# Two-layer hybrid decoder trunk: most weights of the second layer are split into high and low part by two DMAs each

## The chip, the cores and the metric

The kernel runs on one core of one Trainium2 chip. The metric is the device time of one execution in microseconds, of that one core. The engines are called PE (TensorE), DVE (VectorE), ACT (ScalarE), POOL (GpSimd) and SP (SyncE).

## The reference

All arrays are float32, with 512 tokens and 1024 channels. Each of two layers does x <- x + (1 + gate) * Mixer(RMSNorm(x) * (1 + scale) + shift), with shift, scale and gate from a conditioning vector, and a last RMSNorm follows. Layer 0 mixes by causal pooling and stick-breaking attention. Layer 1, where the change lies, is a gated short convolution:

```python
def odd_mixer(h, w_in, conv_w, conv_b, w_out):
    s = h.shape[1]
    proj = h @ w_in                                        # 1024 -> 8192
    gb, gc, u, gate = jnp.split(proj, [D_CONV, 2 * D_CONV, 3 * D_CONV], axis=-1)
    u = gc * u
    up = jnp.pad(u, ((0, 0), (CONV_WIDTH - 1, 0), (0, 0)))
    conv = conv_b + sum(up[:, j:j + s] * conv_w[j] for j in range(CONV_WIDTH))
    y = gb * conv * jax.nn.silu(gate)
    return y @ w_out                                       # 2048 -> 1024
```

## The kernel before

Channels lie on the 128 partitions and the 512 tokens along the free axis. Every operand of a product is held as two float32r tiles, a high part (the value rounded to float32r) and a low part (the rest). `mm3` (L195) makes one product of three matmuls: high weight by high h, high weight by low h, low weight by high h. A weight unit is a 128x1024 tile, eight 128x128 blocks for one output tile of 128 channels by 512 tokens, so a unit is 24 matmuls of 512 columns.

The weights come as a stream of units in the order in which PE uses them (`units`). `load_upto` (L71) issues the load of a unit into a `raw` tile, a ring of three, from SP. `split_upto` (L78) makes the two parts with `hilo` (L58): ACT casts raw to `whi` (L60) and DVE subtracts it from raw into `wlo` (L61); `whi` and `wlo` are rings of three. `next_unit` (L92) is called when the program comes to a unit's products; it splits two units ahead and loads three ahead. Four units at the start of layer 1 are special: three of them go into tiles that attention no longer needs (`vw`), because their products run together, k outside, first on the tokens 0 to 255 and then on 256 to 511 (`layer1`, L745).

Layer 1 has 80 units. Sixteen blocks j of four units (gc, u, gate and gb: `mtile`, L201) each give one y tile; after block 7 the first half of the output projection follows (8 units, `outproj`), and after block 15 the second half (8 units, `outproj_norm`), whose last two units run by token halves under the statistics of the last norm. In a block ACT copies gc out of PSUM (L768), DVE multiplies it with u into a tile whose 16 leading columns POOL sets to zero (L771, L772), DVE does the convolution (L775, L780), ACT takes the SiLU (L783), DVE multiplies (L785, L786), and the result is split into yh and yl by `hilo`. The product tiles rotate over three PSUM banks.

At the end of layer 0, ACT splits the transposed attention weights (`ah`, `al`) and the y tiles of the pooling branch and of the last heads, and casts the weights of the output projection; then the sums of squares give the scale `u` of the new norm, and ACT and DVE make h of layer 1 by k (`hh` L181, `hl` L184), by token halves.

PE and SP run in program order. On ACT, DVE and POOL, apart from the start and a few marked instructions, a scheduler orders the instructions at build time.

Of the kernel before, what the change touches and what calls it, by code (L numbers as in the profile page):

```python
# [7 lines left out]
F32 = mybir.dt.float32  # L8
# [10 lines left out]
P = 128  # L19
# [6 lines left out]

# columns of the packed small parameters
C_G = 0
# [9 lines left out]
class Trunk:  # L38
    def __init__(self, ctx, tc, io):
        self.tc, self.nc, self.io = tc, tc.nc, io  # L40
        pool = lambda name, bufs, **kw: ctx.enter_context(tc.tile_pool(name=name, bufs=bufs, **kw))
        self.c1 = pool("c1", 1)
        self.wp = pool("wp", 2)
        self.yp = pool("yp", 9)
        self.ap = pool("ap", 1)
        self.tp = pool("tp", 2)
        self.pm = pool("pm", 3, space=PSUM)
        self.pz = pool("pz", 5, space=PSUM)
        self.units = []
        self.loaded = 0  # L50
        self.split_done = 0
        self.used = 0

# [1 line left out]
    def t512(self, tag, n=S, bufs=2):  # L55
        return self.tp.tile([P, n], F32, tag=tag, name=tag, bufs=bufs)

    def hilo(self, hi, lo, src, eng=None, ordered=False):  # L58
        """hi = fp32r(src), lo = src - hi."""
        a = self.nc.scalar.copy(out=hi, in_=src)  # L60
        b = (eng or self.nc.vector).tensor_tensor(out=lo, in0=src, in1=hi.bitcast(F32), op=ALU.subtract)  # L61
        if ordered:
            self.tc.keep_in_program_order(a)
            self.tc.keep_in_program_order(b)

# [1 line left out]
    def add_unit(self, src, cols=1024, lo_eng=None):  # L67
        self.units.append(dict(src=src, cols=cols, lo_eng=lo_eng, dst=None))
        return len(self.units) - 1

    def load_upto(self, n):  # L71
        while self.loaded < min(n, len(self.units)):
            u = self.units[self.loaded]
            u["raw"] = self.wp.tile([P, 1024], F32, tag="raw", name="raw", bufs=3)
            self.nc.sync.dma_start(u["raw"][:, : u["cols"]], u["src"])
            self.loaded += 1

    def split_upto(self, n, ordered=False):  # L78
        while self.split_done < min(n, len(self.units)):
            self.load_upto(self.split_done + 1)  # L80
            u = self.units[self.split_done]
            c = u["cols"]
            if u["dst"] is None:
                hi = self.wp.tile([P, 1024], F32R, tag="whi", name="whi", bufs=3)
                lo = self.wp.tile([P, 1024], F32R, tag="wlo", name="wlo", bufs=3)
            else:
                hi, lo = u["dst"]
            self.hilo(hi[:, :c], lo[:, :c], u["raw"][:, :c], u["lo_eng"], ordered)
            u["w"] = (hi, lo)
            self.split_done += 1  # L90

    def next_unit(self, ahead=2):  # L92
        i = self.used
        self.split_upto(i + 1)
        self.load_upto(i + 3)
        self.split_upto(i + 1 + ahead)
        self.load_upto(i + 4)
        self.used += 1
        return self.units[i]["w"]

# [1 line left out]
    def ada_load(self, layer, part, kt, early=None):  # L102
# [31 lines left out]

# [1 line left out]
    def square(self, kt, sl, out=None):  # L136
# [8 lines left out]
    def rstd(self, ps, rs, sl):  # L145
        """1 / sqrt(ps / D + EPS): a table's estimate and a Newton step."""
        nc = self.nc
        n = sl.stop - sl.start
        y = rs[:, sl]
        nc.scalar.activation(y, ps, AF.Abs_reciprocal_sqrt, bias=self.eps, scale=1.0 / D)  # L150
        v = self.t512("sgp")[:, :n]
        r = self.t512("sgp")[:, :n]
        nc.scalar.activation(r, y, AF.Square)
        if n == S:
            nc.scalar.activation(v, ps, AF.Identity, bias=self.heps, scale=-0.5 / D)
        else:
            nc.vector.tensor_scalar(v, ps, -0.5 / D, -0.5 * EPS, ALU.mult, ALU.add)
        nc.vector.tensor_tensor(out=r, in0=r, in1=v, op=ALU.mult)
        nc.vector.scalar_tensor_tensor(y, r, 1.5, y, ALU.add, ALU.mult)
        return y  # L160

    def warm(self, n):
        """Keep the array busy before the products start, so that its clock is up."""
        ps = self.zbank()
        for _ in range(n):
            self.nc.tensor.matmul(ps, self.zero[:, :P], self.zero, start=True, stop=True)

    def preload_rsqrt(self, after):
        """Bring the table in before the statistics need it."""
        n = after.shape[0]  # L170
# [17 lines left out]
    def make_h(self, layer, kt, rstd, sl):  # L188
        """h = x * rstd * A + m as fp32r halves, A = g * (1 + scale), m = shift."""
        t = self.h_scale(layer, kt, rstd, sl)  # L190
        self.h_hi(layer, kt, t, sl)
        self.h_lo(layer, kt, t, sl)

# [1 line left out]
    def mm3(self, ps, wh, wl, xh, xl, first, last):  # L195
# [5 lines left out]
    def mtile(self):  # L201
        """One [128 channels, 512 tokens] tile of the input projection."""
        wh, wl = self.next_unit()
# [25 lines left out]
    def x_add(self, layer, mt, ps, sl=slice(0, S)):  # L229
        """x += gate * ps."""  # L230
        x = self.x[mt][:, sl]
# [17 lines left out]
    def outproj_norm(self, layer, ys, late=None):  # L249
        """The second half of the output projection, with the sums of squares of the new x.  # L250

        The last two tiles go by token halves, so that the first half's statistics are
        worked out under the products of the second. Returns rstd of the first half and
        a function that gives that of the second.
        """
        acc = []
# [60 lines left out]

# [1 line left out]
    def qk_post(self, ps, which):  # L319
# [21 lines left out]

    # column offsets of the row blocks of the scores and of the transposed weights
    ZOFF = {3: 0, 2: 512, 0: 896, 1: 1024}
    TOFF = {0: 0, 1: 512, 3: 896, 2: 1024}

    def attn_z(self, par):
# [5 lines left out]
        for blocks in ((3,), (2, 0), (1,)):  # L352
# [11 lines left out]
            for i in blocks:  # L364
# [6 lines left out]
                )  # L371
                # running products from the right; they stay 1 where the mask is 1
                r = fw[:, o : o + n][:, ::-1]
                nc.vector.tensor_tensor_scan(r, r, self.mask[:, S - n :][:, ::-1], 1.0, ALU.mult, ALU.max)  # L374
        # the last column of each row block is masked, so the neighbour it meets doesn't matter
        nc.vector.tensor_tensor(out=sw[:, :1279], in0=sw[:, :1279], in1=fw[:, 1:], op=ALU.mult)
# [51 lines left out]

# [1 line left out]
    def pool_u(self, ps, j):  # L430
# [21 lines left out]
    def pool_group(self, g, ps_in, sgs):  # L452
        """Per-group map of the pooled channels; returns two y tiles."""
        nc = self.nc
# [16 lines left out]

# [1 line left out]
    def run(self):  # L473
# [12 lines left out]
        nc.gpsimd.memset(self.zero, 0.0)  # L486
        # 1 in the last block's columns k >= q, 0 before
        self.mask = c1.tile([P, S], mybir.dt.bfloat16, name="mask")
# [16 lines left out]

    # order in which the pool tiles are worked on: the widest windows first
    POOLS = (6, 7, 4, 5, 2, 3, 0, 1)
# [38 lines left out]
    def start(self):  # L546
        """Statistics of x, h, and the first products as h comes in, with k outside:
        V of heads 0-7 and the first q, k and gate tiles."""
        nc, io = self.nc, self.io
        full = slice(0, S)  # L550
        crow = self.crow
        # silu(c), then in every partition
        sg = self.ap.tile([P, 1024], F32, tag="s", name="csg", bufs=2)[0:1]
# [64 lines left out]
    def layer0(self):  # L618
# [5 lines left out]
        self.vs = self.ap.tile([P, 4, 1024], F32R, tag="vs", name="vs")  # L624
        # the low parts of k meet the high parts of q: the other rows stay zero
        self.kl = {}
# [33 lines left out]
        for kind, j in self.seq:  # L660
# [47 lines left out]
            else:  # L708
                # y tiles in the order in which they come
                if j == 0:  # L710
                    ys = [yp[i] for i in self.POOLS[:4]] + [ya[i] for i in range(4)]
                    self.outproj(0, ys, lambda mt: self.ada_next(2))
                else:
                    def late():
                        av(7, 1)
                        ys[7] = ya[7]
                        self.preload_rsqrt(st["yt"][:, 0:1])
                        # the first units of the next layer take the place of V
                        vs = self.ap.tile([P, 4, 1024], F32R, tag="vs", name="vw")
# [15 lines left out]
    def plan_l1(self):  # L735
        io = self.io
        self.l1_first = len(self.units)
        for g in range(2):
            for j in range(8 * g, 8 * g + 8):
# [5 lines left out]
    def layer1(self):  # L745
        nc = self.nc
        ha, hb = slice(0, 256), slice(256, S)
        ra = self.ra
        # the first four tiles, by token halves and with k outside
        ws = [self.next_unit(0) for _ in range(4)]  # L750
# [44 lines left out]
        ra, second = self.outproj_norm(1, ys)  # L795
        # final_g goes in on ScalarE, so that GpSimd can share the last products
        fg = lambda k: self.cst[:, C_FG + k : C_FG + k + 1]
# [81 lines left out]
```

## Time and profile before

| what | us |
|---|---|
| span of the profiled execution, first to last instruction | 901.8 |
| times of two executions | 904.85 and 906.72 |
| median of them | 905.79 |
| PE busy | 878.9 |
| DVE busy | 578.5 |
| ACT busy | 354.5 |
| POOL busy | 74.2 |

The page gives the span of the profiled execution and no further time of its own; the two device times are 3.1 and 4.9 us above that span, their median 4.0 us. In the timelines the first column is the start in us from the span's start and the second the length in us. Matmuls overlap: one of 512 columns is shown with 0.39 us but a new one starts every 0.23 us. "out<-in" names tiles without their numbers; "x" and a number is a count.

### The profile page before, as it was taken

What the parts mean: (1) busy time and instruction counts of PE and PEld (TensorE: products, weight loads), DVE (VectorE), ACT (ScalarE), POOL (GpSimd) and SP (SyncE); (2) the same over time, 40 slices, a digit from 0 to 9 for tenths busy, and PEclk for the clock granted to TensorE, in tenths of its full rate; (3) what the DMA queues carried; (4) which work ended last, traced back from release to release, by engine and by line L of the source; (5) the groups of instructions that cost most, each with busy time, mean ns of one, the idle gap of its engine ahead of it and who ended that gap; (6) DMA issues with size and microseconds to landing.
All of it is one profiled execution on the core that took longest, in us unless ns stands there. A gap on an engine that the chain in (4) does not pass through costs nothing.

```text
span 901.8 us, 10787 instructions
## 1 busy us (share of the span) xinstructions
PE 878.9 (97%) x4172; PEld 730.7 (81%) x4172; DVE 578.5 (64%) x803; ACT 354.5 (39%) x552; POOL 74.2 (8%) x114
## 2 busy tenths in 40 slices
PE   8899999999999999999999999999999999999995
PEld 3678788888888888888998888888888888888884
DVE  6989889788878688595675455555334444444445
ACT  6247655656311556564443222222122222222332
POOL 3323202012000012020000000000000000000002
PEclk9999999999999999999999999999999999999998
DMA  9651222223777221213413333333322222332202
GB/s 337 243 175 63 85 71 72 82 78 133 253 259 280 94 71 59 65 64 117 164 48 116 118 116 117 117 117 120 114 94 94 94 93 96 104 105 94 93 24 94
DMA packets 30869, 106.69 MB, mean 118 GB/s; under 512 B 3425, under 2 KB 3553, under 8 KB 30818
## 3 DMA queue, kind: packets, MB, share of 16 engines
q1 hardware_dynamic: 30530, 105.48, 34.1%
q8 instruction: 33, 0.54, 0.2%
q10 hardware_dynamic: 288, 0.52, 0.2%
q14 instruction: 18, 0.15, 0.1%
HBM read 103.90 MB, written 2.10 MB: 118 GB/s over the span
## 4 chain that ended last, share of the span: by engine, by line
PE 85%; DVE 10%; ACT 2%; issue 1%; DMA 1%; SPq 0%; DVEq 0%; ACTq 0%
PE m L197 25%; PE m L198 25%; PE m L199 25%; DVE t L175 2%; DVE ring L114 2%; PE av L403 2%; PE z L390 2%; DVE f L374 1%; PE z L360 1%; PE z L359 1%; PE zb L733 1%; PE zb L732 1%; PE zb L731 1%; PE zb L198 1%; PE zb L199 1%
## 5 line engine op out<-in xcount | busy, mean ns | idle before, releaser
L60 ACT CAST whi<-raw 128x1024 fp32r<-128x1024 f32 (+2 forms) x146 | 151.0, 1036 | 416.7 <-PE m L198 322.2
L197 PE MATMUL m<-hh,whi 128*128 128x512 f32 x776 | 303.7, 391 | 0.6 <-DVE yt L414 0.6
L199 PE MATMUL m<-hh,wlo 128*128 128x512 f32 x776 | 302.2, 389 | 0.0
L198 PE MATMUL m<-hl,whi 128*128 128x512 f32 x776 | 302.2, 389 | 0.0
L61 DVE TENSOR_TENSOR wlo<-raw,whi 128x1024 fp32r<-128x1024 f32 (+1 forms) x138 | 166.4, 1206 | 118.3 <-ACT whi L60 112.1
L197 PEld LDWEIGHTS m<-hh,whi 128*128 128x128 f32 x776 | 145.7, 188 | 30.5 <-DVE yt L414 0.8
L199 PEld LDWEIGHTS m<-hh,wlo 128*128 128x128 f32 x776 | 145.6, 188 | 30.5
L198 PEld LDWEIGHTS m<-hl,whi 128*128 128x128 f32 x776 | 145.8, 188 | 29.4
L197 PE MATMUL m<-yh,whi 128*128 128x512 f32 (+1 forms) x288 | 105.7, 367 | 0.0
L198 PE MATMUL m<-yl,whi 128*128 128x512 f32 (+1 forms) x288 | 105.3, 365 | 0.0
L199 PE MATMUL m<-yh,wlo 128*128 128x512 f32 (+1 forms) x288 | 105.2, 365 | 0.0
L232 DVE SCALAR_TENSOR_TENSOR x<-m,small,x 128x512 f32<-128x512 f32 (+1 forms) x36 | 24.8, 691 | 63.7 <-PE m L199 63.7
L368 POOL TENSOR_SCALAR_AFFINE_SELECT s<-s 128x128 f32<-128x128 f32 x64 | 41.9, 677 | 273.5 <-ACT s L363 273.5
L197 PEld LDWEIGHTS m<-yh,whi 128*128 128x128 f32 x288 | 54.3, 189 | 8.9
L198 PEld LDWEIGHTS m<-yl,whi 128*128 128x128 f32 x288 | 54.3, 189 | 8.8
L199 PEld LDWEIGHTS m<-yh,wlo 128*128 128x128 f32 x288 | 54.3, 189 | 8.7
L374 DVE TENSOR_TENSOR_SCAN f<-f,mask 128x512 f32<-128x512 f32 (+1 forms) x64 | 52.3, 846 | 0.0
L772 DVE TENSOR_TENSOR u<-m,t 128x512 f32<-128x512 f32 x16 | 11.1, 692 | 56.0 <-PE m L199 49.6
L60 ACT CAST yh<-t 128x512 fp32r<-128x512 f32 x40 | 24.8, 621 | 46.4 <-DVE t L447 21.0
L785 DVE TENSOR_TENSOR t<-t,m 128x512 f32<-128x512 f32 x15 | 10.3, 689 | 50.3 <-PE m L199 50.3
L114 DVE CUSTOM_DVE_ANT_0 araw<-araw,cbc,cst 128x1024 f32<-128x1024 f32 x32 | 40.5, 1279 | 2.3 <-DMA araw<-in_ada 2.3
L771 POOL MEMSET u<- 128x16 f32 x16 | 1.8, 112 | 423.3 <-DVE t L780 347.5
(168 smaller groups left out, 973.1 us busy)
## 6 DMA issues: line engine op xcount, KB each, us to landing
raw<-in_w1m SPq DMA_DIRECT2D x64, 512.0 KB, 3.3
raw<-in_w0m SPq DMA_DIRECT2D x37, 512.0 KB, 3.3
araw<-in_ada SPq DMA_DIRECT2D x32, 512.0 KB, 4.5
ring<-in_ada SPq DMA_DIRECT2D x16, 512.0 KB, 5.1
raw<-in_w0o SPq DMA_DIRECT2D x16, 512.0 KB, 4.4
raw<-in_w1o SPq DMA_DIRECT2D x16, 512.0 KB, 3.2
raw<-in_w0s SPq DMA_DIRECT2D x8, 448.0 KB, 4.5
x<-in_x SPq DMA_DIRECT2D x8, 256.0 KB, 4.1
```

Of the source, the lines that this page charges most:

```text
L60: a = self.nc.scalar.copy(out=hi, in_=src)
L61: b = (eng or self.nc.vector).tensor_tensor(out=lo, in0=src, in1=hi.bitcast(F32), op=ALU.subtract)
L114: ins = nc.vector.tensor_tensor_reduce(raw, raw, self.cbc, 1.0, self.cst[:, b : b + 1], ALU.mult, ALU.add, col)
L175: self.nc.vector.scalar_tensor_tensor(t, self.x[kt][:, sl], self.adacol(layer, 1, kt), rstd, ALU.mult, ALU.mult)
L197: mm(ps, wh, xh, start=first, stop=False)
L198: mm(ps, wh, xl, start=False, stop=False)
L199: mm(ps, wl, xh, start=False, stop=last)
L232: self.nc.vector.scalar_tensor_tensor(x, ps[:, sl], self.adacol(layer, 2, mt), x, ALU.mult, ALU.add)
L368: nc.gpsimd.affine_select(out=sw[:, d], in_=sw[:, d], pattern=[[-1, P]], compare_op=ALU.is_gt, fill=0.0, base=0, channel_multiplier=1,)
L374: nc.vector.tensor_tensor_scan(r, r, self.mask[:, S - n :][:, ::-1], 1.0, ALU.mult, ALU.max)
L390: nc.tensor.transpose(ps[:, do : do + P], sw[:, so : so + P], self.ident)
L403: self.nc.tensor.matmul(ps[:, kb * P :], vs[:, kb, c : c + P], t[:, o : o + w], start=(n == 0 and kb == 0), stop=(n == 1 and kb == 3),)
```

## The change

All units from the fifth of layer 1 on (`by_dma`, 76 units) are no longer loaded into `raw`. POOL issues a DMA that reads the float32 weights from HBM and writes them as float32r into the high tile. ACT copies the high tile, times -1, into the low tile. POOL then issues a second DMA that reads the same weights again and adds them to the low tile, which so becomes weight minus high part. DVE has no part in it. The pairs of tiles rotate over five places: three are the rings `whi` and `wlo`, two are the rings `s` and `f` that attention used in layer 0 (tiles named `ws` and `wf`). For these units the split runs three units ahead and the load four.

```diff
+    def wpair(self):
+        return tuple(self.wp.tile([P, 1024], F32R, tag=t, name=t, bufs=3) for t in ("whi", "wlo"))
+
+    def wpair_far(self):
+        self.far_pairs += 1
+        if self.far_pairs % 5 < 3:
+            return self.wpair()
+        return tuple(self.ap.tile([P, 1280], F32R, tag=t, name="w" + t, bufs=2) for t in "sf")
...
     def load_upto(self, n):
         while self.loaded < min(n, len(self.units)):
             u = self.units[self.loaded]
+            if self.loaded >= self.by_dma:
+                u["w"] = u["dst"] or self.wpair_far()
+                self.nc.gpsimd.dma_start(u["w"][0][:, : u["cols"]], u["src"])
+                self.loaded += 1
+                continue
...
     def split_upto(self, n, ordered=False):
...
+            if self.split_done >= self.by_dma:
+                hi, lo = u["w"]
+                self.nc.scalar.activation(lo[:, :c], hi[:, :c].bitcast(F32), AF.Copy, scale=-1.0)
+                self.nc.gpsimd.dma_start(lo[:, :c], u["src"], accum_op=ALU.add)
+                self.split_done += 1
+                continue
...
     def next_unit(self, ahead=2):
         i = self.used
         self.split_upto(i + 1)
         self.load_upto(i + 3)
-        self.split_upto(i + 1 + ahead)
-        self.load_upto(i + 4)
+        far = i + 1 + ahead >= self.by_dma
+        self.split_upto(i + 1 + ahead + far)
+        self.load_upto(i + 4 + far)
...
         self.l1_first = len(self.units)
+        self.by_dma = self.l1_first + 4
```

The change moves line numbers: L103 and L104 of the changed kernel are the negating copy and the adding DMA, L88 is the rounding load; L60 becomes L61, L218 L239, L413 L434, L181 L202, L768 L790 and L783 L805.

On ACT, at the end of layer 0, where the y tiles of the pooling branch (`yh`) and the transposed weights of the last head (`ah`) are split, there stands before:

```order
L60 CAST ah<-z 128x256 [waits PE_49]
L218 ACTIVATE sgp<-m 128x512 [waits DVE_49]
L60 CAST yh<-t 128x512
L60 CAST yh<-t 128x512 [waits DVE_49]
L60 CAST whi<-raw 128x1024 [waits DMAHW0_49,PE_49,Activation_49]
L218 ACTIVATE sgp<-m 128x512 [waits PE_49]
L413 COPY yt<-av 64x512 [waits PE_49]
L60 CAST ah<-z 128x512 [waits DVE_49,PE_49,Activation_49]
L60 CAST ah<-z 128x512 [waits PE_49]
L60 CAST ah<-z 128x256 [waits PE_49]
L60 CAST whi<-raw 128x1024 [waits DMAHW1_49,PE_49]
L60 CAST yh<-t 128x512 [waits DVE_49] x2
```

and at the same place now:

```order
L61 CAST yh<-t 128x512
L103 ACTIVATE wf<-ws 128x1024 [waits DMASW0_49,Activation_49]
L61 CAST yh<-t 128x512 [waits DVE_49]
L61 CAST whi<-raw 128x1024 [waits DMAHW0_49,PE_49]
L239 ACTIVATE sgp<-m 128x512 [waits PE_49]
L434 COPY yt<-av 64x512 [waits PE_49]
L61 CAST ah<-z 128x512 [waits DVE_49,PE_49,Activation_49]
L61 CAST ah<-z 128x512 [waits PE_49]
L61 CAST ah<-z 128x256 [waits PE_49]
L61 CAST whi<-raw 128x1024 [waits DMAHW1_49,PE_49]
L103 ACTIVATE wf<-ws 128x1024 [waits DMASW2_49]
L61 CAST yh<-t 128x512 [waits DVE_49] x2
```

Two negating copies for the units 7 and 8 of layer 1 now stand in ACT's row there, each behind a wait for a rounding load. Two more stand a little later, between the instructions that make h of layer 1 (`hh`):

```order
L202 ACTIVATE hh_115<-t,small 128x256 [waits DVE_49]
L103 ACTIVATE wlo<-whi 128x1024 [waits DMASW4_49,PE_49]
L160 ACTIVATE u_3960<-x_85 128x256 [waits DVE_49]
L202 ACTIVATE hh_116<-t,small 128x256 [waits DVE_49]
L202 ACTIVATE hh_117<-t,small 128x256 [waits DVE_49]
L103 ACTIVATE wlo<-whi 128x1024 [waits DMASW5_49,PE_49]
L202 ACTIVATE hh_118<-t,small 128x256 [waits DVE_49]
```

where before there was no weight among the first eight `hh`:

```order
L181 ACTIVATE hh_115<-t,small 128x256 [waits DVE_49]
L139 ACTIVATE u_3955<-x_85 128x256 [waits DVE_49]
L181 ACTIVATE hh_116<-t,small 128x256 [waits DVE_49]
L181 ACTIVATE hh_117<-t,small 128x256 [waits DVE_49]
L181 ACTIVATE hh_118<-t,small 128x256 [waits DVE_49]
```

The casts of the fifth and sixth unit, which stood among the second eight, are gone from there. In the blocks of layer 1 POOL had one instruction of a block, the memset L771; its row in one block and a little more is now:

```order
L88 DMA whi<-in_w1m 128x1024 [waits DMASW2_49,PE_49]
L88 DMA whi<-in_w1m 128x1024 [waits DMASW3_49,PE_49]
L104 DMA wlo<-in_w1m 128x1024 [waits DMASW4_49,Activation_49]
L793 MEMSET u 128x16 [waits DVE_49,Pool_49]
L104 DMA wlo<-in_w1m 128x1024 [waits DMASW5_49,Activation_49]
L88 DMA whi<-in_w1m 128x1024 [waits DMASW6_49,PE_49]
L104 DMA wlo<-in_w1m 128x1024 [waits DMASW7_49,PE_49,Activation_49]
L88 DMA ws<-in_w1m 128x1024 [waits DMASW0_49,PE_49]
L88 DMA ws<-in_w1m 128x1024 [waits DMASW1_49,PE_49]
L104 DMA wf<-in_w1m 128x1024 [waits DMASW2_49,Activation_49]
```

The loads wait for PE to be through with the pair's last unit, the adding DMAs for ACT's copy, and all of them stand in one row. On ACT a block is now, in its repeating form:

```order
L790 COPY t<-m 128x512 [waits PE_49,Activation_49]
L103 ACTIVATE wf<-ws 128x1024 [waits DMASW2_49]
L103 ACTIVATE wf<-ws 128x1024 [waits DMASW4_49,DMASW3_49,PE_49]
L805 ACTIVATE sga<-m 128x512 [waits PE_49,Activation_49]
L103 ACTIVATE wlo<-whi 128x1024 [waits DMASW5_49]
L61 CAST yh<-t_4754 128x512 [waits DVE_49]
L103 ACTIVATE wlo<-whi 128x1024 [waits DMASW0_49,PE_49]
L790 COPY t<-m 128x512 [waits PE_49,Activation_49]
```

In place of each cast of raw weights stands a negating copy at nearly the same position, and DVE's row is the old one without its subtractions of weights. PE's row has the same matmuls in the same order, with other weight tiles.

## Rows read from the trace of the kernel before

**Rows 1.** The page, part 1: busy time, share of the span, instructions.

```profile
span 901.8 us, 10787 instructions
...
PE 878.9 (97%) x4172; PEld 730.7 (81%) x4172; DVE 578.5 (64%) x803; ACT 354.5 (39%) x552; POOL 74.2 (8%) x114
```

**Rows 2.** Busy time by stretch: the units of layer 1 with 512 columns.

```profile
core 0: us, PE busy (x) PEld busy (x) DVE busy (x) ACT busy (x) POOL busy (x), PEclk, DMA share, GB/s
474.00:885.00 411.00, 411.00 (x1847) 341.75 (x1847) 187.83 (x232) 114.42 (x141) 1.68 (x15) 1.00 0.30 100
```

**Rows 3.** Waits of PE, whole span: waited for, us in total, times, longest.

```profile
PE zb L613 <- ACT hh L181: 7.1, 8, 2.0
...
PE zb L143 <- ACT u L139: 1.9, 1, 1.9
...
PE m L197 <- DVE yt L414: 0.6, 1, 0.6
```

**Rows 4.** Timeline of DVE in the first output projection of layer 1.

```profile
648.98 0.75 DVE L232 SCALAR_TENSOR_TENSOR x<-m,small,x 128x512 f32<-128x512 f32 x1 [3.36 <-PE m L199]
654.42 0.75 DVE L232 SCALAR_TENSOR_TENSOR x<-m,small,x 128x512 f32<-128x512 f32 x1 [3.35 <-PE m L199]
```

**Rows 5.** The split of weights in layer 1: durations in ns; mean ns.

```profile
L61 DVE TENSOR_TENSOR wlo<-raw,whi x71: 1217/1224/1227, 475.6 to 856.6; 128x1024 fp32r<-128x1024 f32 x71
...
L60 ACT CAST whi<-raw 128x1024 fp32r<-128x1024 f32 x73 | 77.0, 1055 | 275.8 <-PE m L198 225.0 <-issue 50.8
```

**Rows 6.** Line L75 from 474 to 860 (min/median/max), and a stretch of layer 0.

```profile
L75 SPq DMA_DIRECT2D raw<-in_w1m x55: 327/328/328, 476.8 to 814.7; - x55
...
DMA to landing us min/median/max: 3.1/3.2/4.7
...
270.00:282.00 12.00, 12.00 (x55) 9.93 (x54) 9.94 (x17) 2.12 (x2) 0.00 (x0) 1.00 0.78 273
```

**Rows 7.** POOL's longest instruction, and the convolution's first step, by line.

```profile
L61 POOL TENSOR_TENSOR wlo<-raw,whi 128x896 fp32r<-128x896 f32 x8 | 19.1, 2387 | 29.5 <-ACT whi L60 29.5
...
L775 DVE TENSOR_SCALAR t<-u,cst 128x512 f32<-128x512 f32 x15 | 8.2, 547 | 0.5
```

**Rows 8.** Timeline at the end of layer 0, ACT, then PE and DVE.

```profile
395.89 0.37 ACT L60 CAST ah<-z 128x256 fp32r<-128x256 f32 x1
...
396.64 0.62 ACT L60 CAST yh<-t 128x512 fp32r<-128x512 f32 x1
399.20 0.62 ACT L60 CAST yh<-t 128x512 fp32r<-128x512 f32 x1 [1.94 <-DVE t L464]
...
404.28 1.06 ACT L60 CAST whi<-raw 128x1024 fp32r<-128x1024 f32 x1 [1.04 <-PE zb L198]
406.38 1.28 ACT L60 CAST yh<-t 128x512 fp32r<-128x512 f32 x2 [1.04 <-DVE t L464]
409.13 0.58 ACT L413 COPY yt<-av 64x512 f32<-64x512 f32 x1 [1.47 <-PE av L403]
...
400.44 1.27 PE L390 MATMUL z<-ident,s 128*128 128x128 f32 x10
407.71 0.74 PE L403 MATMUL av<-ah,vs 128*128 128x512 f32 x4
```

**Rows 9.** Timeline at the start of layer 1, ACT, DVE and PE.

```profile
451.31 0.51 ACT L181 ACTIVATE hh<-t,small 128x256 fp32r<-128x256 f32 x1 [0.41 <-DVE t L175]
451.73 0.40 ACT L139 ACTIVATE u<-x 128x256 f32<-128x256 f32 x1
452.89 0.91 ACT L181 ACTIVATE hh<-t,small 128x256 fp32r<-128x256 f32 x2 [0.76 <-DVE t L175]
...
448.30 0.48 DVE L232 SCALAR_TENSOR_TENSOR x<-m,small,x 128x256 f32<-128x256 f32 x1
...
450.49 0.28 PE L199 MATMUL m<-yh,wlo 128*128 128x256 f32 x1
450.61 0.28 PE L197 MATMUL m<-hh,vw 128*128 128x256 f32 x1
```

More of the change, by code (lines that the diff above doesn't have):

```diff
@@ L50, in __init__ @@
         self.loaded = 0
+        self.far_pairs = 0
         self.split_done = 0
@@ L82, in split_upto @@
             c = u["cols"]
[L83 to L87, printed above, removed]
+            if self.split_done >= self.by_dma:
[4 more added lines that the diff above has]
+                continue
+            hi, lo = u["dst"] or self.wpair()
             self.hilo(hi[:, :c], lo[:, :c], u["raw"][:, :c], u["lo_eng"], ordered)
```

## The prediction

> **What bounds the kernel now.** I read the page's busy times first, then the busy times by stretch, then the waits of PE, then single timelines. PE is busy for 878.9 of 901.8 us [rows 1], and in the stretch in which 74 of the 76 changed units run and the first halves of the last two, from 474 to 885 us, it is busy for all 411.0 us at a granted clock of 1.00, the higher of its levels, while DVE has 187.8, ACT 114.4, POOL 1.7 us of work and the DMA engines are used at a share of 0.30 [rows 2]. A busy PE could hide matmuls that are stretched by late operands, so two more views are needed. In the list of PE's waits, which is short, the largest is 7.1 us for h of layer 0; the reader sees beside it 1.9 us in the last norm and 0.6 us for an attention result, and no wait for a weight [rows 3]. And two neighbouring output tiles end exactly 5.44 us apart (654.42 - 648.98) [rows 4]: 24 matmuls, 0.2267 us each. So PE sets the pace in layer 1, and nothing that DVE, ACT or SP do there is on the path. 5.44 us per unit is the budget in which every other resource has to do its share for one unit.
>
> **The change part by part.** PE keeps its matmuls: 76 units x 24 = 1,824, in the same order. The sum on the path therefore starts at 0.
>
> Removed: 76 subtractions on DVE at 1.224 us [rows 5], 93 us of busy time, all of it beside PE; worth 0 on the path. 76 loads on SP at 0.33 us of issue each [rows 6]; worth 0. ACT trades 76 casts of 1.055 us [rows 5] for 76 copies of the same 128x1024 elements; 0.
>
> Added on POOL: 152 issues, two per unit. The trace has no DMA issued by POOL. The nearest rows bound one issue: 0.33 us, what the same kind of instruction takes on SP [rows 6], and 2.39 us, POOL's longest instruction [rows 7]. Two of them take 0.7 to 4.8 us of 5.44. I take 1.0 us for one, nearer to the DMA row; hidden on POOL, which has 1.7 us of other work in 411 [rows 2].
>
> Added on the DMA engines: the weights are read twice, and the second transfer also reads the tile to which it adds. Price of a plain transfer of a unit: in a busy stretch 273 GB/s came at a share of 0.78 [rows 6], 350 GB/s at a share of 1, so 524,288 bytes take 1.50 us of all engines. A rounding or an adding transfer is not in the trace. For the rounding load I take 1.50 us, as it reads and writes what the plain one does; its upper end is 3.0, as if rounding were a second pass. For the adding one the lower end is 1.50 (the second read is free) and the upper 4.50 (two reads and a write, one after the other); I take 3.0, two passes. A unit then costs 4.5 us of the 5.44, from 3.0 to 6.0 with the rounding at its near end. (The eight loads of conditioning weights in the first blocks add 1.5 / 4 = 0.4 us to a unit for as long as they last.) At 4.5 it is hidden; the cover is gone above 5.44.
>
> The Trainium skill, "Collectives: The Full Stack", section "The bandwidth ceiling: the fold count and why AG ≠ RS ≠ AR", measured the ratio of a copying to a reducing transfer as 1.93 and puts it down to the two source reads; by it the adding transfer would be an estimated 2.9 us and the unit 4.4 us. No run here shows it.
>
> Added as latency: a pair of tiles is free when PE ends unit n-5 and needed at the start of unit n, 4 x 5.44 = 21.8 us later. In between come an issue (1.0), the landing of the rounding load (3.2 in the median for a plain one, 4.7 at most [rows 6]), ACT's copy (1.05), a second issue (1.0) and the adding transfer (3.2 + 1.5 more for the second pass = 4.7): 11.0 us, which leaves 10.8. POOL's row is in order, so an issue also stands behind the one before it; but all wait for the same march of PE, and the spare 10.8 us is two units. On ACT the copies stand between instructions that empty PSUM. In a block, the copy for the second unit loaded after gc was emptied can run 5.44 + 1.0 + 3.2 + 1.05 = 10.7 us after that, and the SiLU behind it is due at 2 x 5.44 = 10.9. If the load lands 3.0 us later, behind a whole adding transfer, the SiLU is 2.8 us late; PE wants its bank three tiles on, with two units (10.9 us) between, so this is covered too.
>
> The two places where the order shows a copy among urgent work have less cover. First, the end of layer 0. The last transposed block of head 14 is split from 395.89 [rows 8], so its tile is free by then; issue and landing bring the load to 395.7 + 1.0 + 3.2 = 399.9. ACT stands there from 397.3 (396.64 + 0.62) and is through at 400.9; the next y cast had started at 399.20, so ACT runs 1.7 us late. The attention weights behind it are cast 1.7 us late, at 405 instead of 403.3 for use at 407.71 [rows 8]: covered. For the second copy the transposes end at 401.7 (400.44 + 1.27), the load lands at about 406.2; ACT gets there at 405.34 + 1.7 = 407.0, so the y casts start at 408.1 instead of 406.38 and the copy of head 15 at 409.4 instead of 409.13 [rows 8]. 0.3 us, with about 2 us to its use: covered. Second, the start of layer 1. The tile of the fifth unit is free at about 448.2, before the x update at 448.30 [rows 9]; the load lands at 452.5. ACT is there after 451.73 + 0.40 = 452.1 and ends the copy at 453.5, where the fourth hh began at 452.89; that hh ends at 454.0, and PE, which began at 450.61 and takes 12 x 0.12 = 1.44 us per k [rows 9], wants it and the hl behind it at 454.9. 0.4 us are left, and each us by which the load lands later than 3.2 after its issue costs up to one. I set 0.5 us for the four places, from 0 to 6 (four times 1.5, the landing at 4.7 instead of 3.2).
>
> Sum: 901.8 + 0.5 = 902.3 us of span; the two times lie 3.1 and 4.9 above the span, 4.0 for their median, so 906.3 us against a median of 905.8.
>
> **The rivals.** (a) The DMA engines become the bound; slower. For it: their work per unit goes from 1.5 us to an unknown 3.0 to 7.5 with both upper ends, the only resource whose upper bound passes the budget. Against it: two passes fit. It decides from 5.44 us per unit on, that is from 3.94 for the adding transfer with the rounding at 1.50. At 1.50 + 4.50 = 6.0 the 10.8 us of cover go in 19 units (0.56 each) and 57 more pay 0.56: +32 us, 938. At 7.5 it would be 71 units x 2.06 = +146.
>
> (b) POOL becomes the bound: the issues take over 2.72 us each. For it: POOL takes 2.39 us for a subtraction that DVE does in about half, and two such fill 4.8 of 5.44; without the weights DVE is still busy for (187.8 - 71 x 1.224) / 411 = 25% of the stretch, and if POOL stood still then, two issues would take 6.4 us: 65 units x 0.96 = +62, 968. Against it: an issue moves no data on POOL. In a block of 21.8 us the only long DVE step with one tensor input is the 0.55 us one of the convolution [rows 7]. The Trainium skill, "SBUF — State Buffer", section "SBUF: two separate sides", warns against just such DMAs: while DVE runs an operation in a two-port mode, POOL can't write the descriptors of its transfers, and such modes are open to steps with one tensor input; that would block a fortieth of the block, and by that rule alone the issues still fit.
>
> (c) The transfers fit, but land late at the four urgent places, and ACT's copies hold up h and y: up to +6 us, 912. For it: each load there may stand behind an adding transfer. Against it: PE has 0.4 to 2 us of cover, and only four copies stand so.
>
> (d) DVE's relief shortens something. The only wait of PE behind layer 1's weights is 1.9 us in the last norm [rows 3], where no weights are split; if it went, 904. Against it: nothing of the change is left to run there.
>
> **How the numbers follow.** The forecast has a chance of 0.70, (a) 0.15, (b) 0.04, (c) 0.07, (d) 0.04. Within 2% (18 us), about what a measurement of this kernel can tell from no change, lie the forecast, (c), (d) all but a hundredth, and of (a) the part where the budget is passed by little, 0.02: 0.82. Slower: 0.17. Faster: 0.01. The range goes from 903, under the times seen, to 938, the near price of (a); what is left out is the dearer part of (a), (b) and a little of (d), together under 0.2. The forecast's own range is 904 to 909.
>
> **What would show it right or wrong.** Right: PE still 100% busy from 474 to 885 with units 5.44 us apart, no wait of PE for a DMA, the DMA share up from 0.30 to about 0.8, DVE's busy time down by 93 us, the time the same. The bounds are settled by the median us from issue to landing of the adding DMA, POOL's time per issue, and ACT's idle time before its negating copies. Wrong: PE waits for `wlo` or `wf` that grow from unit to unit, with a DMA share near 1 (a) or POOL without a gap (b); or PE waits at 396 to 416 and 450 to 460 alone (c).

## The result and the profile after

The changed kernel takes 980.55 us (980.1 and 981.0) against 905.79 us: a ratio of 1.084 with a 95% interval from 1.082 to 1.086. Slower by 75 us, where no change was forecast and the range ended at 938.

The page of the changed kernel; part 2 in 40 slices of 24.5 us:

```profile
span 979.3 us, 10837 instructions
...
PE 908.5 (93%) x4172; PEld 746.3 (76%) x4172; DVE 491.4 (50%) x727; ACT 351.8 (36%) x552; POOL 183.7 (19%) x266
...
PE   7899999999999999999999989879999898898795
...
DMA  8742222244772212544367776767676767675753
...
q0 software_dynamic: 21888, 79.70, 35.0%
```

Against [rows 1] the span is 77.5 us longer, more than the 75 us of the times: in every execution with both numbers on record the time is 1.6 to 1.8 us over its own span (981.0 and 979.3 here), so the profiled execution of before, with 901.8, was a shorter one than the two that were timed. PE's busy time is up by 29.6 us with the same 4,172 matmuls, so the rest, 47.9 us, is new idle time of PE (70.8 us now, 22.9 before). DVE has lost 87.1 us and POOL has 109.5 us more. In the right half neither PE nor the DMA engines are full. Queue q0 is POOL's: its packets take 35.0% of the 16 engines' span, 342.8 us, or 4.51 us for each of the 76 units.

Busy time in a stretch inside layer 1, columns as in [rows 2]:

```profile
500.00:940.00 440.00, 393.07 (x1608) 315.96 (x1607) 86.54 (x132) 91.98 (x112) 97.62 (x147) 0.93 0.70 166
```

PE was busy for all of the stretch in [rows 2]; here it lacks 46.9 of 440.0 us, its granted clock is 0.93 where it was 1.00, and the DMA engines stand still for 30% of the time on average. POOL is busy for 97.62 us, a fifth. So none of these is saturated, and the time is lost to waiting for one another. Who waits for whom stands in the list of waits over the whole span (waited for, us in total, times, longest):

```profile
POOL wlo L104 <- ACT wlo L103: 226.6, 42, 9.2
ACT wlo L103 <- DMA whi<-in_w1m: 164.0, 27, 9.2
POOL wf L104 <- ACT wf L103: 138.0, 26, 9.7
...
PE m L218 <- ACT yh L61: 12.6, 2, 6.7
PE m L220 <- DMA wlo<-in_w1m: 11.5, 6, 2.6
PE m L218 <- ACT sga L805: 11.4, 4, 3.8
PE m L218 <- ACT t L790: 10.1, 4, 3.4
```

POOL stands 364.6 us (226.6 + 138.0) at the adding DMA (L104) waiting for ACT's negating copy, and ACT stands at that copy waiting for a rounding load. The loads themselves wait for PE seven times in the whole run (their line is shown below), six of them up to 493 us, while the stream starts, and once after that, for 0.6 us. The four waits of PE shown sum to 45.6 us, nearly all of its new idle time: 11.5 for an adding DMA, and 34.1 for ACT's other work, the y casts and the copies and SiLUs that empty PSUM, which stand in ACT's row behind copies that wait.

The timelines of POOL, and of ACT with one row of DVE, show the loop. Columns: start, duration, engine, line, operation, count, and in brackets the idle time before it and what ended it.

```profile
610.62 0.87 POOL L104 DMA_DIRECT2D wf<-in_w1m  x1 [8.15 <-ACT wf L103]
611.22 1.39 POOL L88 DMA_DIRECT2D whi<-in_w1m  x2
619.33 0.89 POOL L104 DMA_DIRECT2D wlo<-in_w1m  x1 [6.72 <-ACT wlo L103]
620.78 0.86 POOL L104 DMA_DIRECT2D wlo<-in_w1m  x1 [0.57 <-ACT wlo L103]
621.34 0.87 POOL L88 DMA_DIRECT2D whi<-in_w1m  x1
...
631.03 0.86 POOL L104 DMA_DIRECT2D wlo<-in_w1m  x1 [8.45 <-ACT wlo L103]
```

```profile
387.14 0.62 ACT L61 CAST whi<-raw 128x512 fp32r<-128x512 f32 x1 [2.68 <-PE m L219]
...
410.43 0.58 ACT L434 COPY yt<-av 64x512 f32<-64x512 f32 x1
...
474.95 0.59 ACT L790 COPY t<-m 128x512 f32<-128x512 f32 x1 [7.74 <-PE m L220]
...
617.87 1.06 ACT L103 ACTIVATE wlo<-whi 128x1024 fp32r<-128x1024 f32 x1 [7.16 <-issue]
...
629.55 1.06 ACT L103 ACTIVATE wlo<-whi 128x1024 fp32r<-128x1024 f32 x1 [9.19 <-DMA whi<-in_w1m]
630.52 0.58 ACT L805 ACTIVATE sga<-m 128x512 f32<-128x512 f32 x1
...
957.53 0.48 DVE L253 SCALAR_TENSOR_TENSOR x<-m,small,x 128x256 f32<-128x256 f32 x1 [0.65 <-PE m L220]
```

A turn goes like this. The adding DMA at 610.62 leaves POOL's row, and only then do the two loads behind it go out, at 611.22, with no wait in brackets: their tiles were free. ACT, idle for 7.16 us, can copy the first at 617.87, and at 619.33 the next adding DMA goes. The second turn runs from there over the load at 621.34 and the copy at 629.55 to 631.03. Two turns, 20.41 us, bring three units: 6.80 us for each, where PE needs 5.44 [rows 4]. The SiLU's instruction at 630.52 (L805) stands behind the second copy.

The same three places in the trace of before, ACT and DVE, and a stretch of the changed kernel:

```profile
385.99 0.62 ACT L60 CAST whi<-raw 128x512 fp32r<-128x512 f32 x1 [2.68 <-PE m L198]
...
473.80 0.59 ACT L768 COPY t<-m 128x512 f32<-128x512 f32 x1 [6.33 <-PE m L199]
...
880.34 0.48 DVE L232 SCALAR_TENSOR_TENSOR x<-m,small,x 128x256 f32<-128x256 f32 x1 [0.73 <-PE m L199]
```

```profile
450.00:500.00 50.00, 50.00 (x320) 45.62 (x319) 25.89 (x55) 19.53 (x33) 7.67 (x14) 1.00 0.48 116
```

Over the whole stream: ACT's first copy out of PSUM in layer 1 begins at 474.95, at 473.80 before. Near the end, DVE's first x update of 256 columns (the seventh of the last eight output tiles) begins at 957.53, at 880.34 before. So 77.2 - 1.15 = 76.0 us go in between, in some 74 units: 5.44 + 76.0 / 74 = 6.47 us a unit. 4.51 / 6.47 is 0.70, the DMA share of the stretch. The start of layer 1 cost nothing: the 1.15 us are there already at 387.14, where 385.99 stood, before the first load goes out on POOL, and from 450 to 500 us PE is busy for all 50.00.

Issue and landing by line (duration in ns and us to landing, min/median/max; L88 is the load, L104 the adding DMA; landing counts all tiles of the line), and between them POOL's idle time before L88 by what ended it (us, times):

```profile
L88 POOL DMA_DIRECT2D whi<-in_w1m x36: 535/835/898, 449.2 to 884.6; - x36
...
  PE m L220: 42.0, 3
  PE zb L220: 9.1, 1
  PE z L411: 4.3, 2
  PE m L219: 0.6, 1
...
DMA to landing us min/median/max: 3.5/6.9/9.1
...
L104 POOL DMA_DIRECT2D wlo<-in_w1m x36: 861/880/907, 454.3 to 892.5; - x36
...
DMA to landing us min/median/max: 5.2/5.5/8.6
```

The adding DMA lands in 5.5 us, and the load, which goes out right behind one, takes 6.9 where a plain load took 3.2 [rows 6].

### The profile page after: what moved, and what is told of

It is laid out like the page before. It is cut to its first block, busy times and chain, and to the rows that moved or that the text cites. A ratio compares the mean times of both kernels' runs of the same rounds, so it can differ in the third digit from the quotient of the medians.

```text
span 979.3 us, 10837 instructions
## 1 busy us (share of the span) xinstructions
PE 908.5 (93%) x4172; PEld 746.3 (76%) x4172; DVE 491.4 (50%) x727; ACT 351.8 (36%) x552; POOL 183.7 (19%) x266
## 4 chain that ended last, share of the span: by engine, by line
PE 44%; issue 33%; DVE 11%; POOL 7%; DMA 2%; ACT 2%; SPq 0%; DVEq 0%; POOLq 0%; ACTq 0%
PE m L220 11%; PE m L218 11%; PE m L219 11%; POOL wlo L104 2%; POOL whi L88 2%; DVE t L196 2%; DVE ring L135 2%; PE av L424 2%; PE z L411 2%; POOL ws L88 2%; POOL wf L104 1%; DVE f L395 1%; DMA wlo<-in_w1m 1%; PE z L381 1%; PE z L380 1%
## 5 line engine op out<-in xcount | busy, mean ns | idle before, releaser
L218 PE MATMUL m<-hh,whi 128*128 128x512 f32 x584 | 233.6, 400 | 10.6 <-ACT t L790 5.4
L220 PE MATMUL m<-hh,wlo 128*128 128x512 f32 x584 | 232.3, 398 | 11.5 <-DMA wlo<-in_w1m 11.5
L219 PE MATMUL m<-hl,whi 128*128 128x512 f32 x584 | 231.5, 396 | 0.0
L218 PEld LDWEIGHTS m<-hh,whi 128*128 128x128 f32 x584 | 112.2, 192 | 35.3 <-ACT t L790 6.2
L103 ACT ACTIVATE wlo<-whi 128x1024 fp32r<-128x1024 f32 x46 | 48.8, 1060 | 229.7 <-DMA whi<-in_w1m 164.0
L61 ACT CAST whi<-raw 128x1024 fp32r<-128x1024 f32 (+2 forms) x70 | 71.0, 1017 | 141.4 <-PE m L219 97.9
L62 DVE TENSOR_TENSOR wlo<-raw,whi 128x1024 fp32r<-128x1024 f32 (+1 forms) x62 | 73.5, 1187 | 45.8 <-ACT whi L61 40.7
L218 PE MATMUL m<-hh,ws 128*128 128x512 f32 x192 | 78.9, 411 | 11.5 <-ACT sga L805 6.8
L218 PE MATMUL m<-yh,whi 128*128 128x512 f32 (+1 forms) x240 | 88.6, 369 | 0.0
L103 ACT ACTIVATE wf<-ws 128x1024 fp32r<-128x1024 f32 x30 | 31.8, 1060 | 144.1 <-DMA ws<-in_w1m 91.9
L220 PE MATMUL m<-hh,wf 128*128 128x512 f32 x192 | 78.0, 406 | 1.3 <-DMA wf<-in_w1m 1.2
L219 PE MATMUL m<-hl,ws 128*128 128x512 f32 x192 | 78.0, 406 | 0.0
L104 POOL DMA_DIRECT2D wlo<-in_w1m x36 | 31.7, 881 | 176.5 <-ACT wlo L103 172.2
L218 PEld LDWEIGHTS m<-hh,ws 128*128 128x128 f32 x192 | 38.1, 198 | 21.5 <-ACT sga L805 7.9
```

The costliest lines, as they stand in the source:

```text
L103: self.nc.scalar.activation(lo[:, :c], hi[:, :c].bitcast(F32), AF.Copy, scale=-1.0)
L104: self.nc.gpsimd.dma_start(lo[:, :c], u["src"], accum_op=ALU.add)
L218: mm(ps, wh, xh, start=first, stop=False)
L219: mm(ps, wh, xl, start=False, stop=False)
L220: mm(ps, wl, xh, start=False, stop=last)
```

## The experiments

Two theories. ORDER: each load is issued too late, behind an adding DMA that waits for ACT, so a chain of latencies comes round once or twice in three units, and what the DMA engines could move doesn't matter. RATE: the transfers themselves are too slow for 5.44 us a unit. A third, POOL's issue as the bound, is out by the page: 97.62 us of work in 440. One execution of the kernel before, beside the first four kernels below, took 903.12 us; the median of fifteen, beside the last three, is 903.95. Where no other count is given, a kernel below was executed once.

**Cut the loop at ACT.** The copy reads a constant instead of the loaded tile, so it waits for no load. All transfers and instructions stay; the low parts are not those of the weights.

```diff
-                self.nc.scalar.activation(lo[:, :c], hi[:, :c].bitcast(F32), AF.Copy, scale=-1.0)
+                self.nc.scalar.activation(lo[:, :c], self.cbc[:, :c], AF.Copy, scale=-1.0)
```

> The copy on ScalarE reads a constant tile of the same shape in place of the high part, so that it no longer waits for the rounding load; every DMA, its bytes and ScalarE's work stay (the low part is then not the rest of the weight). Theory ORDER (the rounding loads stand in GpSimd's row behind adding DMAs that wait for ScalarE's copy of a load that has only just been issued; the DMA queue runs dry in each turn): the turn is broken, a unit falls from about 6.4 us to the 5.44 us of TensorE, time 904 to 912. Theory RATE (the DMA engines need over 5.44 us for the two transfers of a unit): nothing changes, 970 to 985.

Measured: 903.85 us. A stretch of it, and a line of POOL's timeline:

```profile
600.00:700.00 100.00, 100.00 (x443) 82.81 (x442) 20.42 (x31) 24.93 (x28) 26.33 (x39) 1.00 0.90 193
```

```profile
708.97 0.55 POOL L88 DMA_DIRECT2D ws<-in_w1m  x1 [2.32 <-PE m L220]
```

PE is busy for 100 of 100 us, at a DMA share of 0.90, and the loads now wait for PE, 75 of the 76: there is a lead again. The transfers fit in 5.44 us; RATE falls for this kernel.

**Change the order alone.** Each load is written ahead of the adding DMA of an earlier unit, and POOL is held to the order of the program in layer 1.

```diff
+        if far:
+            self.load_upto(i + 5)
         self.split_upto(i + 1 + ahead + far)
...
-            self.layer1()
+            with tc.manual_schedule(engines={POOL}):
+                self.layer1()
```

> Only the order: the load of unit n+1 is issued ahead of the adding DMA of unit n throughout, and GpSimd keeps that order in layer 1. ORDER: a turn of about 9.5 us then carries two units, 4.7 us each, so TensorE sets the pace again, 904 to 920. RATE: 970 to 985. A third way (ScalarE's copies, which wait for loads, hold up its PSUM copies): between, 920 to 960.

Measured: 905.40 us. The same kernel, executed eleven times more:

> The kernel of e3_load_first timed against the one before the change. ORDER with TensorE as the bound: the same within 0.4% (ratio 0.998 to 1.004). A gain of over 0.4% would mean that the work taken from VectorE was on the path after all; a loss of over 0.4% that the order leaves waits.

The median is 904.53 us against 903.95, a ratio of 1.0006 with an interval from 0.9997 to 1.0016. POOL's timeline and a wait of ACT in the first of these runs, and a stretch of the second:

```profile
705.07 0.55 POOL L88 DMA_DIRECT2D whi<-in_w1m  x1 [3.35 <-PE m L222]
...
710.50 0.55 POOL L88 DMA_DIRECT2D ws<-in_w1m  x1 [3.46 <-PE m L222]
...
715.94 0.55 POOL L88 DMA_DIRECT2D ws<-in_w1m  x1 [3.26 <-PE m L222]
```

```profile
ACT wlo L103 <- DMA whi<-in_w1m: 127.0, 34, 7.6
```

```profile
474.00:885.00 411.00, 411.00 (x1847) 341.84 (x1847) 103.23 (x158) 112.56 (x139) 106.44 (x161) 1.00 0.89 193
```

The same DMAs with the same bytes: the loads go out 5.43 and 5.44 us apart, each when PE frees a tile. PE is busy for all 411.00 us as in [rows 2], and DVE has 103.23 us of work there instead of 187.83. So the whole loss hangs on POOL's order. In a block ACT's row keeps the order of the changed kernel; at the end of layer 0, where nothing was lost, the scheduler moved the two copies away. The third way, named in the expectation, falls too: ACT's copies still wait for loads in front of its other work, 127.0 us for `whi` where it was 164.0, and PE loses nothing by it.

**The worse order.** POOL is held to program order without the swap, which gives strictly one adding DMA, then one load: a whole turn for each unit instead of two for three.

```diff
-            self.layer1()
+            with tc.manual_schedule(engines={POOL}):
+                self.layer1()
```

> The opposite order, kept by hand in layer 1: the adding DMA of unit n always ahead of the load of unit n+1, so that each turn carries one unit. ORDER: a turn with one unit is a landing of 6.7 us behind one adding DMA, the copy of 1.06 and about 0.9 us of issues, 8.6 us a unit instead of 6.4: 905.8 + 76 x 3.16 - 10.8 = 1135, range 1090 to 1170. RATE: the two transfers need the same engines' time in either order, 970 to 985.

Measured: 1100.75 us. POOL's timeline and a stretch:

```profile
640.51 0.86 POOL L104 DMA_DIRECT2D wf<-in_w1m  x1 [6.67 <-ACT wf L103]
641.06 0.87 POOL L88 DMA_DIRECT2D whi<-in_w1m  x1
...
682.20 0.87 POOL L104 DMA_DIRECT2D wf<-in_w1o  x1 [7.18 <-ACT wf L103]
```

```profile
500.00:1040.00 540.00, 423.44 (x1596) 325.33 (x1596) 85.70 (x131) 94.86 (x112) 95.28 (x144) 0.91 0.55 131
```

Five units take 682.20 - 640.51 = 41.69 us, 8.34 each, at a DMA share of 0.55. The time is inside the band that ORDER gave. It also shows that holding POOL to an order is not what helped above: the order itself did.

**A faster second transfer.** The adding DMA only writes; POOL's order stays that of the changed kernel. The low parts are then the weights themselves.

```diff
-                self.nc.gpsimd.dma_start(lo[:, :c], u["src"], accum_op=ALU.add)
+                self.nc.gpsimd.dma_start(lo[:, :c], u["src"])
```

> The second DMA writes the rounded weights again without adding (no low part), same instructions in the same order. By the packets (328 ns adding, 174 ns rounding) it is 1.2 us shorter. ORDER: the turn of 20.4 us for three units loses 3.7 us, 5.6 us a unit, 910 to 925. RATE: the two transfers then need 2.8 us a unit, 904 to 908. It measures what the adding costs within the loss.

Measured: 903.68 us. From the page, and POOL's timeline:

```profile
q0 software_dynamic: 21888, 79.70, 27.9%
...
whi<-in_w1m POOLq DMA_DIRECT2D x36, 512.0 KB, 4.9
```

```profile
701.91 0.53 POOL L104 DMA_DIRECT2D wlo<-in_w1m  x1 [7.07 <-ACT wlo L103]
...
708.94 0.54 POOL L104 DMA_DIRECT2D wlo<-in_w1m  x1 [5.01 <-ACT wlo L103]
...
717.96 0.53 POOL L104 DMA_DIRECT2D wf<-in_w1m  x1 [6.64 <-ACT wf L103]
```

ORDER's price missed: 910 us at least was expected, and by the bands alone the time speaks for RATE (904 to 908). But the loop is still there, with waits of 5 to 7 us for ACT in each turn; two turns now take 717.96 - 701.91 = 16.05 us, 5.35 for each of three units, just under PE's 5.44. The turns lost more than was allowed for: the issue fell from 0.88 to 0.53 us, and the landing of a load, which is the one in the turn, from 6.9 to 4.9 in the median. That is 2 x (0.35 + 2.0) = 4.7 us where 3.7 was allowed. So by itself this run doesn't tell the theories apart. It prices the transfers: 27.9% of 902.0 us is 251.7, 3.31 for a unit of two rounding transfers, so 1.66 for one, and 4.51 - 1.66 = 2.85 for an adding one.

**The load back on SP.** SP loads the raw weights as before, ACT casts and negates them, POOL issues only the adding DMA.

```diff
-            if self.loaded >= self.by_dma:
...
-                hi, lo = u["w"]
+                hi, lo = u["w"] = self.wpair_far()
+                self.nc.scalar.copy(out=hi[:, :c], in_=u["raw"][:, :c])
```

> The high part is made as before the change (plain load from SyncE, cast on ScalarE); the low part as after it (negating copy, adding DMA). ORDER: GpSimd's row holds only adding DMAs, nothing waits behind them, 904 to 912. RATE: the bytes are the same and the adding transfer too, 960 to 985.

Measured: 909.38 us, 6.3 over the one execution of the kernel before. ACT's timeline at the start of layer 1:

```profile
447.79 1.05 ACT L97 CAST ws<-raw 128x1024 fp32r<-128x1024 f32 x1 [1.02 <-DMA raw<-in_w1m]
...
453.63 0.51 ACT L197 ACTIVATE hh<-t,small 128x256 fp32r<-128x256 f32 x1
...
479.20 0.59 ACT L785 COPY t<-m 128x512 f32<-128x512 f32 x1 [8.13 <-PE m L215]
```

With the loads in another queue there is no loop, and the adding DMAs alone cost nothing in the steady part: PE is busy for all of 500 to 880 us. What is lost is lost before it: the first copy out of PSUM comes at 479.20 instead of 473.80, 5.4 us late. Of these, 1.6 are there before any changed instruction runs (387.62 for the cast at 385.99), so 3.8 belong to the start of layer 1, where ACT casts weights ahead of `hh`, PE waits 1.8 us for an `hh` and its granted clock is 0.93 from 450 to 475. It is this cost, ACT's copies among urgent work, that the prediction looked for at the seams. The queue of the adding DMAs stands by itself here: 26.6% of 907.7 us, 3.18 for each, more than the 2.85 got by difference.

**How far the engines are from the bound.** The kernel with the loads first, and in 60 projection units PE leaves out the products of the high weights with the low part of h (8 of 24 matmuls).

```diff
-            self.mm3(ps, wh[:, c], wl[:, c], self.hh[k], self.hl[k], k == 0, k == KT - 1)
+            if self.used <= self.by_dma:
+                self.mm3(ps, wh[:, c], wl[:, c], self.hh[k], self.hl[k], k == 0, k == KT - 1)
+            else:
+                mm(ps, wh[:, c], self.hh[k], start=k == 0, stop=False)
+                mm(ps, wl[:, c], self.hh[k], start=False, stop=k == KT - 1)
```

> As e3_load_first, but the 60 units of the input projection that are split by DMA leave out the product of high weights and low h, so that TensorE needs 3.63 us for such a unit: it lays bare what the DMA path sets next. If the engines' time decides (share 0.92 of 5.44 us in e3_load_first, 5.0 us a unit): 60 x 0.44 less, 870 to 885. If the turn of two units decides (about 9.4 us): 855 to 868. If neither does, 60 x 1.81 less: 796.

Measured: 867.51 us. From the waits of PE, and a stretch:

```profile
PE m L235 <- DMA wlo<-in_w1m: 21.8, 20, 2.4
...
PE m L235 <- DMA wf<-in_w1m: 16.5, 15, 1.9
```

```profile
680.00:740.00 60.00, 49.68 (x196) 37.18 (x197) 14.65 (x21) 17.11 (x21) 17.72 (x28) 0.97 0.96 219
```

The time is at the upper edge of the band given for the turn and 2.5 us under that given for the engines, so by itself it leans to the turn. The rows don't settle it. PE waits 38.3 us (21.8 + 16.5) for adding DMAs over the run, but it does so in the worse order too, for 129.8 us at a share of 0.55. In the stretch the DMA share is 0.96, where it was 0.70 in the loop: that speaks for the engines. POOL again waits 213.9 us at the adding DMAs for ACT's copies: that speaks for the turn. 37.0 us less in 60 units is 0.62 each: 5.44 - 0.62 = 4.8 us a unit, against 3.63 for 16 matmuls. So at 4.8 us, 0.6 below PE's pace, the engines are all but full. Whether they or the turn set that pace stays open, but rival (a) was near.

## Why the prediction was wrong

**PE as the bound, and the budget:** right. Where nothing is late, units are 5.44 us apart and PE is 100% busy at 1.00, in the run with the loads first.

**Removed, worth 0:** right. DVE's busy time fell by 87 us in all, the subtractions alone by 92.9 (from 166.4 to 73.5, where 93 were worked out), and the run with the loads first, which has lost it too, has a ratio of 1.0006.

**POOL's issues, 1.0 us each:** nearly right: 0.54 to 0.91 in the rows, with DVE at work for 86.54 of the 440 us. Rival (b) is out.

**The DMA engines, 1.50 + 3.0 = 4.5 us a unit:** right in the sum as a mean of the changed kernel, 4.51, of which 1.66 for the rounding and, by difference, 2.85 for the adding one. With the loads first the same packets take 41.1% of 903.7 us, 4.89 a unit, so the cover is 0.55 us and not 0.9. Rival (a) is not the cause: with the same bytes PE doesn't wait once the order is changed. The Trainium skill, "Collectives: The Full Stack", section "The bandwidth ceiling: the fold count and why AG ≠ RS ≠ AR", measured AllGather, which copies, at 1.93 times the rate of ReduceScatter, which adds. Here 2.85 us stand against 1.50 for a plain one (1.9), which agrees, and against 1.66 for a rounding one (1.7), somewhat less.

**Added as latency:** this is the step that failed. It took the latency of one unit, 11.0 us, and held it against the 21.8 us from the free tile to its use. On POOL's row it said that "an issue also stands behind the one before it; but all wait for the same march of PE, and the spare 10.8 us is two units". They don't wait for PE: loads did so seven times in the whole run, once after 493 us, and adding DMAs waited 364.6 us for ACT. Since the row has the load for a later unit behind the adding DMA of an earlier one, which waits for the copy of a load issued just before it, the chain is closed: adding DMA, load, landing, copy, next adding DMA. A closed chain has a rate, and no lead covers a rate that is too low; it only puts off the first wait: PE is still busy for all of 450 to 500 us and falls short from there on. None of the four rivals holds this loop, and their signs failed accordingly: PE waits, but with the DMA share at 0.70 and POOL idle for most of the time.

The numbers for it stood in the prediction. The POOL row shown ahead of it has the loads in groups of two and one between adding DMAs, so two turns for three units. By the step's own terms a turn is 1.0 + 1.0 for the issues, 3.2 + 3.0 for a load that lands behind an adding transfer, and 1.05 for the copy: 9.25 us; two make 18.5, or 6.2 us a unit, 0.7 over the budget and some +54 us in 74 units, less the 10.8 us of cover. The delay of 3.0 us was even considered, but for one SiLU, once. The rows give the turns 8.71 and 11.70 us, 6.8 us a unit, and the whole stream 6.47.

**Late at the four places, 0.5 us:** the seams cost nothing that the rows show. The copy of head 15, forecast at 409.4, began at 410.43, and 409.3 without the 1.15 us that were there before. (Two sums on the way are slightly off: 401.7 + 1.0 + 3.2 is 405.9 and not 406.2, and 448.2 + 4.2 is 452.4 and not 452.5; the time doesn't hang on them.) But rival (c)'s mechanism, ACT's row held up by a copy that waits, works inside the blocks: ten of PE's waits, 34.1 of 45.6 us, come by ACT. It is how the loop reaches PE and not the cause, as the run with the loads first shows.

**What the clock adds:** not in the prediction. PE's granted clock is 0.93 on average in the stretch in which it stands still again and again, and the same matmuls take 29.6 us more of busy time. How much of the loss is the clock and how much the waiting can't be separated here, since a slower matmul that fills a wait need not cost anything; the turn on POOL explains the pace without it.

## What to carry to other kernels

When an instruction stream waits for another engine, look for what stands behind the waiting instruction in the same row and whether its result feeds the next wait: if so, work out the time of one turn and the units it brings, and compare that with the budget as you would a busy time. A lead in buffers hides a latency only if the issue runs ahead; here a load written ahead of the waiting DMA, and kept there, was worth 76 us with not a byte changed. A share of 0.70 on the engine that everyone suspects, beside idle time on all others, was the sign of the loop here.

## What the runs showed of the hardware

- A rounding DMA of 512 KB costs the 16 engines 1.66 us, an adding one 2.85 (by difference) to 3.18 (beside plain loads), where the plain one of the kernel before comes to 1.50. These are means over a kernel: the pair took 4.51 us at a share of 0.70 and 4.89 with the loads first, at 0.89.
- POOL's issues begin 0.56 us apart in places (620.78 and 621.34) though a row may give each 0.87: such rows overlap and must not be added up.
- In one queue a load takes 6.9 us to land behind an adding transfer; with the copy cut loose, where loads go out some 4 us after the last adding DMA (708.97 behind 704.92) and the share was 0.90, the median for `whi` was 4.1. That the queue is served in order fits these numbers, but wasn't tested by itself.
